# Even layer's out-projection on one Trainium2 core: operand blocks loaded by a casting DMA, low halves made by a negation and an adding DMA from GpSimd

## The chip, the cores and the metric

The kernel runs on one core of one Trainium2 chip. The metric is device time in microseconds, the median of several executions. The core's engines are named as in the profile: PE is TensorE (matmuls), PEld its weight loads, DVE VectorE, ACT ScalarE, POOL GpSimd and SP SyncE. A queue that issues DMAs is written with a q, as SPq.

## The reference, cut to what matters

The reference is a chain of four residual layers over one sequence of 1024 tokens with 1024 features in fp32: a gated linear recurrence (A), a latent attention (M), an even layer (E) and an odd layer (O), and a last normalisation. Layer E joins two branches and projects them back:

```
y_a = attn.reshape(b, s, DA_WIDTH) * silu(g_a)
...
y_b = rmsnorm(y, ssd_norm_w)
return concatenate([y_a, y_b], axis=-1) @ w_out
```

`y_a` comes from a differential attention, `y_b` from a state-space scan (SSD). Each has 1024 features, so `w_out` is 2048 by 1024 and its product is a sum of two parts: `y_a` by the upper half and `y_b` by the lower half. The change lies in how the blocks of `y_a` and `y_b` are brought into SBUF for this product.

## The kernel before, in words

**The matmul in three products.** TensorE multiplies operands of a rounded type, float32r (F32R in the code). To keep fp32 accuracy, every operand x is held as a high half, x rounded to float32r, and a low half, x minus that. `split` (line 545) makes them: ACT copies x into the high tile, which rounds it, and DVE subtracts the high tile from x into the low tile. A product is then three matmuls (`mm3`): high by high, high by low, low by high.

**The out-projection.** `out_proj` (line 853) takes the two parts with their sources in DRAM: `yA_d` for the attention, `yB_d` for the scan. Each is stored with 8 rows of 128 features, by 1024 tokens. The 1024 output features are done in four column groups c of 256. `PLANS` (line 802) gives each group a form: PPSS for the first part, PSSP for the second. P is a plain product (`plain`, line 889): four blocks, for output half b and token half h, of 8 row tiles by 3 matmuls, 24 matmuls each; the block for (b, h) = (0, 0) comes first, then (0, 1), (1, 0), (1, 1). S is a seven-product form on sums and differences of the operand blocks: 7 by 4 by 3, 84 matmuls. The sums are made from loads of their own (`load_sums`, tiles `tq`).

**The quads.** Both forms read quads. A quad is a quarter of the operand, 512 features by 512 tokens, as two pairs of tiles `yh` (high) and `yl` (low), each tile 128 partitions by 2 rows by 512 tokens. `load_quad` (line 804) loads one:

```
E.sync.dma_start(out=b.bitcast(F32), in_=src[k:k + 2, :, hs(h)].rearrange("k p s -> p k s"))
split(a, b, b.bitcast(F32))
```

So the fp32 block, 512 KB, lands in the tile `b` of the low half, ACT rounds it into `a`, and DVE subtracts in place. A part's first P needs all four quads, in the order (0,0), (1,0), (0,1), (1,1) of feature half and token half, which is 8 tile pairs. The first S of a part drops quad (0,1), and the last P of the second part loads it again, 2 more pairs. In all `load_quad` runs its inner body 8 + 8 + 2 = 18 times. No other layer calls it.

**What sets the order.** The kernel is written as a list of operations; `schedule` (line 296) plays them through a model of the engines and writes out a fixed order for every engine, so each engine runs its instructions strictly in that order and waits on semaphores. An operation's place follows from when its inputs are ready in the model, and among ready ones from its place in the list. `price` (line 253) gives a DMA 460 ns on the engine that issues it, whichever that is; line 377 lets it land at the earliest 2 us later, all DMAs one after another at 330 bytes per ns. A tile is taken from its class when the first operation that writes it is placed (`can_alloc`, line 319). Tiles `yh`, `yl`, `xr` and those of the scan share the class `c4`, 38 slots of 4 KB per partition; `yh` and `yl` have at most 16 each.

**Around the change.** SP issues all DMAs of the kernel before. POOL has few instructions: the additions of squares (`sumsq`, line 613) where the planner gives them to it, into `gacc` for the scan's normalisation and `acc` for the next layer's, and the power -1/2 behind every normalisation (`far_rstd`, line 582, and `next_norm`, line 644). The scan's result reaches `yB_d` only behind such a power. Every instruction is issued at line 431, so the profile names that line for all, and they are told apart by tile names: `ops` is the PSUM tile of the out-projection, `mm`, `yo`, `tp` those of the scan, `xr` the residual stream to which DVE adds each finished `ops`.

Of the kernel before, what the change touches and what calls it, by code (L numbers as in the profile page):

```python
# [10 lines left out]
F32 = mybir.dt.float32  # L11
F32R = mybir.dt.float32r
AF = mybir.ActivationFunctionType
ALU = mybir.AluOpType
# [420 lines left out]
def tile_kernel(ctx: ExitStack, tc: tile.TileContext, A, cc, out, stages="AMEO", dump=False):  # L435
    nc = tc.nc
    N4, N2, NW, NX = 38, 12, 9, 24
    E = Program()
# [3 lines left out]
    hs = lambda h: slice(h * HALF, (h + 1) * HALF)  # L442
# [102 lines left out]
    def split(hi, lo, src):  # L545
        splits((hi, lo, src))

    def splits(*items):
        for hi, lo, src in items:
            E.scalar.copy(hi, src)  # L550
        for hi, lo, src in items:
            E.vector.tensor_tensor(out=lo, in0=src, in1=hi.bitcast(F32), op=ALU.subtract)
# [251 lines left out]
    def load_quad(src, kq, h):  # L804
        hi, lo = [], []
        for j in range(2):
            a, b = T("yh", [128, 2, HALF], F32R), T("yl", [128, 2, HALF], F32R)
            k = kq * 4 + j * 2
            E.sync.dma_start(out=b.bitcast(F32), in_=src[k:k + 2, :, hs(h)].rearrange("k p s -> p k s"))
            split(a, b, b.bitcast(F32))  # L810
            hi.append(a)
            lo.append(b)
        return hi, lo
# [39 lines left out]
    def out_proj(parts, kind, near={}):  # L853
# [45 lines left out]
        for pi, (w_ap, nk, src) in enumerate(parts):  # L899
# [20 lines left out]
            def need(*which):  # L920
                for q in which:
                    if q not in quads:
                        quads[q] = load_quad(src, *q)
# [777 lines left out]
```

## Time and profile before

| | before |
|---|---|
| median of 3 executions | 2289.41 us (2288.76 to 2289.72) |
| the profiled execution's own time | 2289.98 us |
| its span, first to last instruction | 2288.2 us |
| PE busy | 2268.0 us |
| DVE busy | 1644.9 us |
| ACT busy | 1340.7 us |
| POOL busy | 113.8 us |
| granted TensorE clock, mean | 0.999 of full speed |
| DMA queue of SP | 207.92 MB, 28.7% of 16 engines' span |

Matmuls are pipelined and their ends are modelled, so PE counts as busy from a matmul's start to its modelled end: gaps shorter than the overlap don't show. The span is 1.8 us shorter than the execution's own time. The out-projection of layer E lies between about 1720 and 1900 us of the span; its loads begin at about 1670 us.

### The profile page before, as it was taken

What the parts mean: (1) busy time and instruction counts of PE and PEld (TensorE: products, weight loads), DVE (VectorE), ACT (ScalarE), POOL (GpSimd) and SP (SyncE); (2) the same over time, 40 slices, a digit from 0 to 9 for tenths busy, and PEclk for the clock granted to TensorE, in tenths of its full rate; (3) what the DMA queues carried; (4) which work ended last, traced back from release to release, by engine and by line L of the source; (5) the groups of instructions that cost most, each with busy time, mean ns of one, the idle gap of its engine ahead of it and who ended that gap; (6) DMA issues with size and microseconds to landing.
All of it is one profiled execution on the core that took longest, in us unless ns stands there. A gap on an engine that the chain in (4) does not pass through costs nothing.

```text
span 2288.2 us, 33162 instructions
## 1 busy us (share of the span) xinstructions
PE 2268.0 (99%) x11994; PEld 1917.2 (84%) x11994; DVE 1644.9 (72%) x3784; ACT 1340.7 (59%) x2778; POOL 113.8 (5%) x145
## 2 busy tenths in 40 slices
PE   8999999999999999999999999999999999999998
PEld 7888888888999888889898888878887878888887
DVE  7677944455777855976776757887879966777875
ACT  6666823433666744576666757586543435777852
POOL 0000011000000001000000000000000021000000
PEclk9999999999999999999999999999999999999999
DMA  6122423222111512312111121263336523111241
GB/s 224 60 80 86 170 88 92 65 97 90 47 53 58 188 65 59 120 38 56 48 48 47 51 60 43 56 173 93 111 131 213 191 74 113 47 56 47 95 164 74
DMA packets 181549, 210.04 MB, mean 92 GB/s; under 512 B 24729, under 2 KB 131445, under 8 KB 181385
## 3 DMA queue, kind: packets, MB, share of 16 engines
q1 hardware_dynamic: 181385, 207.92, 28.7%
q8 instruction: 94, 1.54, 0.3%
q14 instruction: 70, 0.57, 0.1%
HBM read 159.50 MB, written 46.28 MB: 90 GB/s over the span
## 4 chain that ended last, share of the span: by engine, by line
PE 96%; DVE 1%; DMA 1%; issue 1%; ACT 0%; SPq 0%; DVEq 0%; POOLq 0%; POOL 0%; ACTq 0%
PE mm L431 53%; PE ops L431 19%; PE sc L431 8%; PE ov L431 6%; PE tps L431 4%; PE yo L431 1%; PE mg L431 1%; PE tp L431 1%; PE nps L431 1%; DMA xT_d<-xe 0%; DMA csb<-cs_d 0%; PE aux L431 0%; DVE yl L431 0%; PE ftp L431 0%; SPq L431 0%
## 5 line engine op out<-in xcount | busy, mean ns | idle before, releaser
L431 PE MATMUL mm<-hT,whi 128*128 128x512 f32 (+1 forms) x3136 | 1001.4, 394 | 0.7 <-ACT hT L431 0.5
L431 PEld LDWEIGHTS mm<-hT,whi 128*128 128x128 f32 x3136 | 578.7, 188 | 119.4 <-issue 1.0
L431 PE MATMUL mm<-hT,wlo 128*128 128x512 f32 (+1 forms) x1568 | 616.3, 394 | 0.0
L431 PEld LDWEIGHTS mm<-hT,wlo 128*128 128x128 f32 x1568 | 294.9, 188 | 62.0 <-issue 1.4
L431 ACT ACTIVATE s<-s,st 128x257 f32<-128x257 f32 (+9 forms) x467 | 301.0, 663 | 73.3 <-DVE st L431 71.2
L431 PE MATMUL ops<-yh,whi 128*128 128x512 f32 x528 | 207.7, 396 | 0.6 <-DVE xr L431 0.6
L431 PE MATMUL ops<-yl,whi 128*128 128x512 f32 x528 | 208.1, 395 | 0.2 <-DVE yl L431 0.2
L431 PE MATMUL ops<-yh,wlo 128*128 128x512 f32 x528 | 207.9, 395 | 0.0
L431 DVE TENSOR_TENSOR pl<-tps,ph 128x512 fp32r<-128x512 f32 (+2 forms) x284 | 143.3, 536 | 79.1 <-ACT ph L431 77.3
L431 ACT CAST ph<-tps 128x512 fp32r<-128x512 f32 (+2 forms) x284 | 120.6, 469 | 106.8 <-PE tps L431 104.8
L431 DVE CUSTOM_DVE_ANT_0 s<-sc,bt 128x256 f32<-128x256 f32 (+3 forms) x320 | 149.6, 493 | 40.1 <-PE sc L431 37.2
L431 DVE TENSOR_TENSOR wlo<-raw,whi 128x512 fp32r<-128x512 f32 (+5 forms) x246 | 160.9, 673 | 21.6 <-ACT whi L431 15.9
L431 PE MATMUL ov<-ph,v 128*128 128x256 f32 (+2 forms) x700 | 159.7, 285 | 0.0
L431 DVE TENSOR_TENSOR xr<-ops,xr 128x512 f32<-128x512 f32 x108 | 74.2, 688 | 111.1 <-PE ops L431 110.9
L431 ACT CAST whi<-raw 128x512 fp32r<-128x512 f32 (+5 forms) x246 | 136.3, 582 | 20.1 <-DVE wlo L431 14.4
L431 PE MATMUL tps<-ident,s 128*128 128x128 f32 x816 | 135.2, 273 | 0.0
L431 PEld LDWEIGHTS ov<-ph,v 128*128 128x128 f32 x700 | 118.2, 189 | 9.8 <-ACT ph L431 1.6
L431 PEld LDWEIGHTS ops<-yh,whi 128*128 128x128 f32 x528 | 99.2, 188 | 24.1 <-DVE xr L431 1.0
L431 PEld LDWEIGHTS ops<-yl,whi 128*128 128x128 f32 x528 | 99.2, 188 | 23.6 <-DVE yl L431 0.6
L431 PEld LDWEIGHTS ops<-yh,wlo 128*128 128x128 f32 x528 | 99.1, 188 | 23.1
L431 PE MATMUL ov<-pl,v 128*128 128x256 f32 (+1 forms) x380 | 116.9, 308 | 0.2 <-DVE pl L431 0.2
L431 PEld LDWEIGHTS tps<-ident,s 128*128 128x128 f32 x816 | 99.2, 140 | 11.9
(318 smaller groups left out, 3999.3 us busy)
## 6 DMA issues: line engine op xcount, KB each, us to landing
raw<-in_w_in_a_dram SPq DMA_DIRECT2D x72, 512.0 KB
yl<-yA_d SPq DMA_DIRECT2D x48, 256.0 KB
raw<-in_w_out_a_dram SPq DMA_DIRECT2D x24, 512.0 KB
xr<-xT_d SPq DMA_DIRECT2D x24, 512.0 KB
raw<-in_w_in_c_dram SPq DMA_DIRECT2D x18, 512.0 KB
xT_d<-xr SPq DMA_DIRECT2D x32, 256.0 KB
yA_d<-y SPq DMA_DIRECT2D x32, 256.0 KB
csb<-cs_d SPq DMA_DIRECT2D x16, 512.0 KB
```

Source lines behind the costliest of these rows:

```text
L431: getattr(getattr(nc, op.eng), op.method)(*[conv(a) for a in op.args], **{k: conv(v) for k, v in op.kwargs.items()})
```

## The change

In `load_quad` alone, three lines replace two. The block is loaded by a DMA that GpSimd issues, from DRAM in fp32 into the high tile `a`, which has the type float32r, so the DMA casts. ACT writes the negative of `a` into the low tile `b`, with a Copy of scale -1. A second DMA of GpSimd reads the same block from DRAM again and adds it to `b`. DVE has no part in it any more.

```
--- before.py
+++ after.py
@@ -806,8 +806,10 @@
         for j in range(2):
             a, b = T("yh", [128, 2, HALF], F32R), T("yl", [128, 2, HALF], F32R)
             k = kq * 4 + j * 2
-            E.sync.dma_start(out=b.bitcast(F32), in_=src[k:k + 2, :, hs(h)].rearrange("k p s -> p k s"))
-            split(a, b, b.bitcast(F32))
+            y = src[k:k + 2, :, hs(h)].rearrange("k p s -> p k s")
+            E.gpsimd.dma_start(out=a, in_=y)
+            E.scalar.activation(b, a.bitcast(F32), AF.Copy, scale=-1.0)
+            E.gpsimd.dma_start(out=b, in_=y, accum_op=ALU.add)
             hi.append(a)
             lo.append(b)
         return hi, lo
```

The tile that is written first is now `a` where it was `b`.

## Rows read from the trace of the kernel before

**Rows 1.** The page, part 1: busy us, share of the span, instructions.

```profile
PE 2268.0 (99%) x11994; PEld 1917.2 (84%) x11994; DVE 1644.9 (72%) x3784; ACT 1340.7 (59%) x2778; POOL 113.8 (5%) x145
```

**Rows 2.** Windows: us, then PE, PEld, DVE, ACT, POOL busy, PEclk, DMA share, GB/s.

```profile
0.00:50.00 50.00, 41.12 (x298) 38.59 (x299) 36.19 (x99) 34.89 (x68) 4.93 (x20) 1.00 0.75 255
...
1700.00:1900.00 200.00, 198.22 (x915) 159.69 (x914) 165.90 (x250) 85.46 (x134) 21.17 (x15) 1.00 0.45 150
...
2250.00:2300.00 50.00, 31.15 (x135) 24.93 (x133) 19.53 (x38) 8.69 (x24) 3.54 (x7) 0.94 0.20 74
```

**Rows 3.** Tile views of yl and yh, 1660 to 1900 us: min/median/max ns.

```profile
L431 ACT CAST yh<-yl x18: 1031/1048/1053, 1700.8 to 1859.8; 128x1024 fp32r<-128x1024 f32 x18
L431 DVE TENSOR_TENSOR yl<-yl,yh x18: 1215/1220/1227, 1703.5 to 1862.3; 128x1024 fp32r<-128x1024 f32 x18
...
L431 SPq DMA_DIRECT2D yl<-yB_d x10: 359/371/1187, 1769.8 to 1831.6; - x10
```

**Rows 4.** Chain of waits, 1741 to 1831 us: start, us, what.

```profile
1741.67 88.06 PE ops L431 x379
```

**Rows 5.** Timeline of ACT, first part's roundings: start, us, instruction, idle before.

```profile
1710.38 2.93 ACT L431 CAST yh<-yl 128x1024 fp32r<-128x1024 f32 x3
...
1721.43 1.05 ACT L431 CAST yh<-yl 128x1024 fp32r<-128x1024 f32 x1
```

**Rows 6.** Timeline of PEld, out-projection's start: 1st, 7th and 43rd load of part one.

```profile
1720.29 0.19 PEld L431 LDWEIGHTS ops<-yh,whi 128*128 128x128 f32 x1
...
1721.57 0.19 PEld L431 LDWEIGHTS ops<-yh,whi 128*128 128x128 f32 x1
...
1736.65 0.19 PEld L431 LDWEIGHTS ops<-yh,whi 128*128 128x128 f32 x1
```

**Rows 7.** Timeline of SP, the second part's quad loads.

```profile
1769.77 0.89 SPq L431 DMA_DIRECT2D yl<-yB_d  x2
...
1793.71 4.54 SPq L431 DMA_DIRECT2D yl<-yB_d  x5
...
1799.37 1.19 SPq L431 DMA_DIRECT2D yl<-yB_d  x1
```

**Rows 8.** Timeline of ACT, the second part's roundings; in brackets the idle time and its end.

```profile
1793.49 1.05 ACT L431 CAST yh<-yl 128x1024 fp32r<-128x1024 f32 x1 [2.80 <-PE ops L431]
1794.88 1.05 ACT L431 CAST yh<-yl 128x1024 fp32r<-128x1024 f32 x1 [0.35 <-PE ops L431]
...
1797.81 1.05 ACT L431 CAST yh<-yl 128x1024 fp32r<-128x1024 f32 x1 [1.35 <-DMA yl<-yB_d]
...
1804.93 1.05 ACT L431 CAST yh<-yl 128x1024 fp32r<-128x1024 f32 x1 [0.96 <-DMA yl<-yB_d]
```

**Rows 9.** Timeline of DVE, second part: additions of the first two finished blocks.

```profile
1817.85 0.68 DVE L431 TENSOR_TENSOR xr<-ops,xr 128x512 f32<-128x512 f32 x1
...
1823.27 0.68 DVE L431 TENSOR_TENSOR xr<-ops,xr 128x512 f32<-128x512 f32 x1
```

**Rows 10.** Windows again, columns as in Rows 2: two stretches full of DMAs.

```profile
1715.00:1720.00 5.00, 4.88 (x24) 3.72 (x23) 5.00 (x6) 3.90 (x6) 0.00 (x0) 1.00 1.03 419
...
1800.00:1805.00 5.00, 5.00 (x23) 4.06 (x22) 3.72 (x4) 2.17 (x3) 0.00 (x0) 1.00 1.04 373
```

**Rows 11.** Timelines of POOL, then SP: sums, a power, the store of yB_d.

```profile
1734.18 1.49 POOL L431 TENSOR_TENSOR gacc<-gacc,sq 128x512 f32<-128x512 f32 x1 [31.90 <-ACT sq L431]
...
1745.37 1.02 POOL L431 TENSOR_TENSOR r<-r,mhalf 128x4 f32<-128x4 f32 x1 [7.12 <-DVE r L431]
...
1756.31 5.37 SPq L431 DMA_DIRECT2D yB_d<-yb  x8
```

## The prediction, made blind

> **What bounds the kernel now.** The page's table of engines comes first: PE is busy for 2268.0 of 2288.2 us, DVE for 72% of the span, POOL for 5% [rows 1]. The windows say where PE's missing 20.2 us lie: 8.9 in the first 50 us, 7.1 in the last 38, and only 1.8 in the 200 us that hold the out-projection, all of it at a granted clock of 1.00 [rows 2]. The chain of waits shows the same from the other side: one run of 379 matmuls in 88.06 us without a wait, 0.2323 us each [rows 4]. So PE sets the end in this stretch, and DVE, busy for 165.9 of those 200 us, is close behind but hidden. Whatever the change takes from DVE can return at most the 1.8 us in which PE stood idle; whatever it makes PE wait is added in full, since matmuls at 0.2323 us each leave nothing to catch up with.
>
> **What it removes.** 18 subtractions of 1.22 us leave DVE, 22.0 us in all [rows 3]. Worth: between 0 and 1.8 us, as above; I take 1.8, since the idle time lies where DVE is full [rows 2]. 18 DMA issues leave SP, 0.36 to 1.19 us each [rows 3]. SP's loads of weights and sums behind them may go out earlier; they are prefetches, so I count 0.
>
> **What it replaces.** ACT's 18 roundings of 1.05 us [rows 3] become 18 negations of the same shape. I take the same 1.05, a gain or loss of 0. What changes is the place: the negation waits for the casting DMA, as the rounding waited for the plain one, and ACT's later work queues behind it.
>
> **What it adds.** The old chain for a tile pair was DMA, ACT 1.05, DVE 1.22. The new one is casting DMA, ACT 1.05, adding DMA. The adding DMA can't start before ACT has finished, so a whole transfer takes the place of 1.22 us, and the operand blocks cross the DMA engines twice: 36 transfers of 512 KB where 18 were. The trace has no DMA from POOL, none that casts and none that adds, so both prices are bounded. From below: DMA engines that are full move 419 GB/s [rows 10], 1.25 us for 524288 bytes. From above, if only one is under way at a time: a quad load issued at 1793.71 released ACT by 1797.81 [rows 7, 8], 4.1 us, and a second stream (the adding DMA also reads its target) 2.4 us more, 6.5 us. The nearest rows are the second part's own loads of the same blocks: ACT was released at 1797.81 and, three loads later, at 1804.93 [rows 8], 2.4 us each. I take 2.4 for the casting DMA and 1.5 times that, 3.6, for the adding one, half way between one stream and two.
>
> The Trainium skill, in "DMA: Bandwidth & Descriptors", section "Anatomy of one DMA — SWDGE (gpsimd) path", gives 2.0 us plus the bytes over 436 GB/s for a DMA that GpSimd generates: as an estimate 3.2 us here alone, and 1.2 for each further one where the fixed part overlaps. By that the second part's sum below would be 14 times 1.2 plus 2, so no stall, or 14 times 3.2, so a stall of 17 us less the cover; no run here shows which.
>
> **First part: late or not.** PE takes up the first tile pair at 1720.29, the second (7th weight load) at 1721.57 and the eighth (43rd) at 1736.65 [rows 6]. ACT's second rounding starts at 1710.38 and the eighth ends at 1722.48 [rows 5]. With negations at the same places, the second adding DMA can start at about 1711.4, and seven of them at 3.6 us end at 1736.6: just in time, 0 us. At the lower bound they wait for ACT; at the upper one they end at 1756.9, 20 us late. In the way are the loads of `xr`: the DMA engines are full here as it is [rows 10].
>
> **Second part: this is where I expect the loss.** Its blocks can only be loaded into slots that the first part's last S form gives free. Two slots were free early, and two loads went out at 1769.77; six more at 1793.71 to 1800.6 [rows 7], after ACT had waited for PE's last use of old tiles [rows 8]. In the new kernel the two early slots go to the high tiles, so two casting DMAs are done early, but everything else, 6 casting and 8 adding DMAs, starts at about 1793.5. PE's first block ended by 1817.85 and its second by 1823.27 [rows 9]; 24 matmuls take 5.6 us [rows 4], so the first began near 1812.1, and the eighth tile pair (19th matmul of the second block) was needed at about 1821.8. That leaves 28.3 us. The transfers need 8 times 3.6 and 6 times 2.4, 43.2 us: 14.9 us late. The planner counts DMAs one after another as well, so it will put a block that reads the early quads, output half 1 by token half 0, in between: 24 matmuls, 5.6 us of cover. Stall 9.3 us.
>
> **The reload** of quad (0,1), two tile pairs for the last P form, is rounded by ACT between 1858 and 1862, the second pair by 1862.3 on DVE [rows 3]. It is outside the rush; two adding DMAs, 7.2 us, delay nothing that I can see: 0, and at 6.5 us each still under 10 us in a stretch of 60 us of PE work that doesn't read it.
>
> **POOL's queue.** POOL gets 36 DMA issues between its own instructions, and a waiting one holds those behind it: an adding DMA waits for ACT, and behind it stand the last sums of squares at 1734.18 and the power at 1745.37, which lead to the store of `yB_d`, issued by 1761.7 [rows 11]. Up to 1793.5, when the slots come free, that chain has 31.8 us to spare, and eight adding DMAs end at 1736.6 by my price: 0 us.
>
> **The sum.** 9.3 of new stall less 1.8 given back is 7.5 us. On the profiled execution's 2289.98 us, which is 0.6 us above the median of the runs shown, this gives 2297.5 us.
>
> **Rivals.**
> - *The transfers keep pace* (35%). With casts at 2.4, the second part fits its 28.3 us and the 5.6 of cover if an adding DMA takes 2.4 us or less, the pace of a plain load. For it: DMA engines at 419 GB/s would need 1.25 us per stream, and the windows after 1805 have room. Then only DVE's relief is left, 2288.2 to about 2290 us.
> - *Adding DMAs cost two streams or more, or run one at a time* (17%). At 4.8 us, twice 2.4, the first part ends at 1745.0, 8.4 late, 2.8 after the cover of one block; the second needs 52.8 us, 24.5 late, 18.9 after cover. With 1.8 back, 2310 us; the upper bounds (6.5 and 4.1) give some 2347.
> - *POOL becomes the bound* (5%). If issues waiting on slots or on ACT hold POOL past 1777, the power comes over 31.8 us late, the `yB_d` chain reaches PE, and each further us is a us lost: 2300 us for 10.
> - *Faster by over 0.2%* (3%). It would take 4.6 us, and PE idles only 4.2 us outside the first 50 and last 38 us of the span. Only another order of the whole plan could do it: about 2284 us.
>
> That the casting DMA doesn't round, or that the low half comes out as zero, would cost accuracy and leave the matmuls and these times as they are.
>
> **How the numbers follow.** The forecast has 40%; its own range, for adding DMAs of 3.2 to 4.2 us, is 2294 to 2303. A difference of 0.2%, 4.6 us, is about what a measurement of this kernel can tell from none. Slower by more: all but 5 of the forecast's 40, with 17 and 5 from the second and third rival, 0.57. Within 0.2%: 35 and 5, 0.40. Faster: 0.03. The range runs from 2287.5, all of DVE's relief and no stall, to 2322, the second rival half way to its bounds; it leaves out the slow end of the one-at-a-time case and the faster plan.
>
> **What would show it.** In the changed kernel's chain of waits, PE's long run of `ops` should break near 1812 to 1830, with DMAs into `yl` as what ended the idle time; the windows there should show the DMA engines full. ACT should show waits on DMAs into `yh`, DVE 22 us less work, POOL 36 issues. I am wrong if PE's busy time stays within 2 us of 2268 and the time with it (the transfers keep pace), if the largest gap lies before 1745 (the first part), or if `yl` is in time and PE waits for something behind POOL.

## The result and the profile after

The changed kernel takes 2346.90 us (median of 4, 2346.65 to 2351.78), before 2289.56 on the same chip: 1.025 times as long, interval 1.0238 to 1.0262, or 57.3 us more. The forecast was 2297.5 with a range up to 2322. The profiled execution took 2351.78 us, 4.9 above the median.

The page of the changed kernel: its span and engines (columns as in [rows 1]):

```profile
span 2350.0 us, 33202 instructions
...
PE 2287.0 (97%) x11994; PEld 1928.1 (82%) x11994; DVE 1624.4 (69%) x3767; ACT 1340.5 (57%) x2778; POOL 147.7 (6%) x180
```

And its DMA queues, the page's third part (packets, MB, share of sixteen engines over the span):

```profile
q1 hardware_dynamic: 176489, 198.49, 26.6%
q0 software_dynamic: 9792, 18.88, 3.8%
```

DVE has lost 20.5 us of work: the 18 subtractions, less one addition of squares that the planner now gives to DVE in place of POOL. ACT has the same as before. POOL has 35 instructions more and a DMA queue of its own, q0, with the 36 new transfers. The span is 61.8 us longer, and 19.0 of these are PE being busy longer. The rest is waiting, as the waits of PE between 1700 and 1960 us show (who waited for whom: us in total, times, longest; `nps` is the PSUM tile of the scan's normalisation, `sqh` its rounded sum of squares, which comes behind POOL's additions, and `whi` the high half of the weights):

```profile
PE ops L431 <- DMA yl<-yB_d: 19.4, 6, 6.4
PE nps L431 <- ACT sqh L431: 12.0, 2, 11.8
PE ops L431 <- ACT whi L431: 4.4, 1, 4.4
PE ops L431 <- DMA yl<-yA_d: 3.8, 1, 3.8
```

With three smaller groups this is 44.3 us, where PE stood idle for 1.8 us in the 200 us of [rows 2]. Where the waits come from is seen on POOL. Its timeline in the second part:

```profile
1862.42 1.21 POOL L431 DMA_DIRECT2D yl<-yB_d  x1 [8.94 <-issue]
1869.18 1.21 POOL L431 DMA_DIRECT2D yl<-yB_d  x1 [5.55 <-ACT whi L431]
1875.94 1.19 POOL L431 DMA_DIRECT2D yl<-yB_d  x1 [5.56 <-issue]
1882.76 1.20 POOL L431 DMA_DIRECT2D yl<-yB_d  x1 [5.63 <-issue]
```

The tile view of `yl`, 1862 to 1895 us, says when these four adding DMAs landed:

```profile
L431 POOL DMA_DIRECT2D yl<-yB_d x4: 1189/1200/1206, 1862.4 to 1882.8; - x4
...
DMA to landing us min/median/max: 6.4/6.5/6.5
```

An adding DMA lands 6.4 to 6.5 us after its issue, and the next starts 6.8 us after the one before: one at a time. POOL idles 5.6 us in between. ACT can't be what it waits for, since the last negation before these issues started at 1853.25 and took 1.06 us; the profile finds no releaser ("issue") for two of the three gaps. Nor are the DMA engines the reason, as the window of the four shows (columns as in [rows 2]):

```profile
1862.40:1889.20 26.80, 16.35 (x48) 11.68 (x48) 7.02 (x12) 2.50 (x4) 4.80 (x4) 0.82 0.52 80
```

They are busy for 0.52 of 26.8 us, 3.5 us for each adding DMA, and idle for the rest. (80 GB/s over 26.8 us is 2.1 MB, the four blocks and little else.)

PE's 19.0 us of longer busy time are in part the clock. After the long gap in the first part it comes back slow. The window of those 10 us (columns as in [rows 2]):

```profile
1750.00:1760.00 10.00, 5.89 (x15) 4.54 (x15) 1.29 (x2) 2.84 (x5) 5.00 (x4) 0.53 0.46 89
```

And the timeline of PE there:

```profile
1754.11 0.79 PE L431 MATMUL nps<-sqh,ones_r 128*128 128x512 f32 x1 [11.76 <-ACT sqh L431]
...
1755.13 0.63 PE L431 MATMUL ops<-yh,whi 128*128 128x512 f32 x1
1755.56 0.63 PE L431 MATMUL ops<-yl,whi 128*128 128x512 f32 x1
```

The granted clock is 0.53 in this window, the lower level of 1.2 GHz, after PE had stood still for 11.76 us, and matmuls follow each other at 0.43 us, where [rows 4] has 0.23.

### The profile page after: what moved, and what is told of

Same layout as the page of the kernel before. It is cut to its first block, busy times and chain, and to the rows that moved or that the text cites. A ratio compares the mean times of both kernels' runs of the same rounds, so it can differ in the third digit from the quotient of the medians.

```text
span 2350.0 us, 33202 instructions
## 1 busy us (share of the span) xinstructions
PE 2287.0 (97%) x11994; PEld 1928.1 (82%) x11994; DVE 1624.4 (69%) x3767; ACT 1340.5 (57%) x2778; POOL 147.7 (6%) x180
## 4 chain that ended last, share of the span: by engine, by line
PE 90%; issue 5%; DMA 2%; DVE 1%; POOL 1%; SPq 0%; ACT 0%; POOLq 0%; DVEq 0%; ACTq 0%
PE mm L431 51%; PE ops L431 16%; PE sc L431 8%; PE ov L431 6%; PE tps L431 4%; PE yo L431 1%; PE mg L431 1%; PE tp L431 1%; PE nps L431 1%; POOL yl L431 1%; SPq L431 0%; DMA xT_d<-xe 0%; DMA csb<-cs_d 0%; PE aux L431 0%; POOL yh L431 0%
## 5 line engine op out<-in xcount | busy, mean ns | idle before, releaser
L431 ACT ACTIVATE sq<-xr 128x512 f32<-128x512 f32 x58 | 36.6, 631 | 135.0 <-DVE xr L431 128.9
```

Of the source, the lines that this page charges most:

```text
L431: getattr(getattr(nc, op.eng), op.method)(*[conv(a) for a in op.args], **{k: conv(v) for k, v in op.kwargs.items()})
```

## The experiments

Three theories stood against each other from the trace: that POOL has room for only one adding DMA at a time (R), that the move itself takes 6.5 us (M), and that POOL waits for ACT in the order that the planner wrote (Q). The expectations put the room down to descriptors, the entries that are written for a transfer; the runs vary the room and don't show what fills it. The kernel sets a scratch size for such DMAs itself, `dynamic_dma_scratch_size=1024`, and R takes that for the room. The ratios are to the kernel before, run beside each version, with medians of 2290.5 to 2291.2 us.

**More room.** The changed kernel, with one number altered:

```
-    nc = bacc.Bacc("TRN2", ..., dynamic_dma_scratch_size=1024)
+    nc = bacc.Bacc("TRN2", ..., dynamic_dma_scratch_size=4096)
```

> The changed kernel with a DMA scratch of 4096 bytes per partition in place of 1024, nothing else. In the changed kernel POOL issues the adding DMAs 6.4 to 6.8 us apart and sits idle in between for nothing that the profile names, while the DMA engines are only half busy. Theory R (the room for descriptors: an adding DMA fills more than half of it, so one is under way at a time, and POOL waits for the one before to land): with four times the room they overlap, each then costs what the DMA engines are busy for it, about half of 6.8, 3.4 us; the time falls from 2347 to between 2292 and 2312. Theory M (the move itself takes 6.5 us, and they run one after another whatever the room): 2340 to 2350. Theory Q (POOL waits for ACT, in the order the planner wrote): 2340 to 2350 too, with POOL's waits put down to ACT.

Measured: 2304.94 us, 1.0065 times before (1.0042 to 1.0088). 42 of the 57 us are gone. POOL's timeline in the second part's rush:

```profile
1809.15 1.20 POOL L431 DMA_DIRECT2D yl<-yB_d  x1 [3.81 <-ACT yl L431]
1814.93 1.20 POOL L431 DMA_DIRECT2D yl<-yB_d  x1 [4.58 <-ACT yl L431]
1817.34 1.19 POOL L431 DMA_DIRECT2D yl<-yB_d  x1 [1.22 <-ACT yl L431]
1819.10 1.18 POOL L431 DMA_DIRECT2D yl<-yB_d  x1 [0.57 <-ACT yl L431]
```

Now they follow at down to 1.8 us, and what POOL waits for is ACT's negation. That 6.5 us is the move's own time is out, and so is Q in this form: both would have left the time as it was. A smaller step of the same number:

> The changed kernel with a DMA scratch of 2048 bytes. With 1024 the time is 2347 (adding DMAs one at a time), with 4096 it is 2305 (DMA engines full, POOL never idle for an unnamed reason). If the room for descriptors is a count of transfers (theory R), twice the room lets two or three adding DMAs overlap, which at a landing time of 6.5 us and 3.3 us of movement each nearly fills the DMA engines: 2305 to 2320, much nearer to 4096 than to 1024. If the gain with 4096 came from other addresses in SBUF or from the plan, 2048 should give no ordered step: 2335 or more is against theory R.

Measured: 2308.27 us (1.0088, 1.0059 to 1.0117). Twice the room brings most of the gain, as R had it. POOL still idles for an unnamed reason in places, here 4.90 us, where the kernel with 4096 has at most 0.3 us of it before an issue in the rush:

```profile
1828.96 1.18 POOL L431 DMA_DIRECT2D yl<-yB_d  x1 [4.90 <-issue]
```

**Cut the adding DMA in two**, with the room of 1024:

```
-            E.gpsimd.dma_start(out=b, in_=y, accum_op=ALU.add)
+            for n in range(2):
+                E.gpsimd.dma_start(out=b[:, n], in_=src[k + n, :, hs(h)], accum_op=ALU.add)
```

> The changed kernel, scratch 1024, with each adding DMA of two rows cut into two of one row, 256 KB each. Theory R: each half takes half the room, so two or three halves are under way at once and the cost per block falls from 6.6 to some 4 to 5 us: 2305 to 2330. Theory M: the same bytes at the same pace, 2343 to 2352, or later by the second DMA's fixed part.

Measured: 2318.63 us (1.0122, 1.0093 to 1.0151). The same bytes in the same room, in smaller pieces, save 28 us.

The traces say more on the room than these times, if issue and landing of every DMA of POOL are put side by side. Count an adding DMA of 512 KB as two and every other (casting, plain, or adding half a block) as one: then with 1024 never more than 3 are under way, in any run, and with 2048 never more than 7, while with 4096 there are up to 11 and no such wait. In the changed kernel 23 stretches of POOL's idle time, 101.5 us in all, end 0.3 us after the landing of an earlier DMA of POOL, whatever the profile names as releaser. What fills the room isn't shown by this: the profiles' pages count the same 272 packets for an adding and for a casting DMA (4896 over 18, below), and 144 for a plain one (2592 over 18).

**Each half of the change alone.** Casting DMA only, in place of the negation and the adding DMA:

```
+            E.sync.dma_start(out=b.bitcast(F32), in_=y)
+            E.vector.tensor_tensor(out=b, in0=b.bitcast(F32), in1=a.bitcast(F32), op=ALU.subtract)
```

> Half of the change: the casting DMA of POOL writes the high tile, SP loads the same block in fp32 into the low tile as before, DVE subtracts in place; no negation, no adding DMA. Theory R: a casting DMA is smaller in descriptors and nothing waits for two transfers in a row, so the operand is in time as before: 2286 to 2296. Against it (any DMA that POOL issues comes late): 2300 or more.

Measured: 2294.87 us (1.0018, 1.0007 to 1.0029). And the adding DMA only, with

```
-            E.gpsimd.dma_start(out=a, in_=y)
+            E.sync.dma_start(out=a.bitcast(F32), in_=y)
+            E.scalar.copy(a, a.bitcast(F32))
```

> The other half: SP loads the block in fp32 into the high tile, ACT rounds it in place and writes its negative into the low tile, POOL's adding DMA adds the block; no casting DMA. Theory R: the adding DMAs alone hold the time, 2332 to 2347. Against it (casting DMAs, which share the room and POOL's queue, carry a third or more of the loss): 2295 to 2328.

Measured: 2351.35 us (1.0265, 1.0234 to 1.0296), all of the loss, and above the range by 4 us. Each of the two has 18 DMAs of POOL of one kind, so their pages price the kinds (columns as above). Casting only, span 2293.3 us:

```profile
q0 software_dynamic: 4896, 9.44, 1.4%
```

Adding only, span 2347.1 us:

```profile
q0 software_dynamic: 4896, 9.44, 2.5%
```

That is 1.4% of 2293.3 us over 18, 1.8 us of all sixteen engines for a casting DMA, and 2.5% of 2347.1 over 18, 3.3 us for an adding one. A landing of 6.5 us is thus about half movement.

**POOL as the issuer, nothing else.** In the kernel before, `E.sync` becomes `E.gpsimd` for the quads' loads:

> The kernel before with one edit: the quads' plain loads are issued by POOL in place of SP; no cast, no adding DMA, ACT rounds and DVE subtracts as before, scratch 1024. It prices the move of 18 DMAs to POOL alone. Theory R: a plain transfer is small in room, nothing follows it but ACT: 2288 to 2293. Against it (POOL's DMAs come late whatever they do): 2298 or more.

Measured: 2291.75 us (1.0005, 0.9996 to 1.0015): no difference that can be told from none. The move to POOL alone isn't the loss. Its queue, span 2287.7 us:

```profile
q0 software_dynamic: 2592, 9.44, 1.2%
```

Over 18 that is 1.5 us of all sixteen engines for a plain DMA of POOL.

**Each part alone.** The new lines under `if src is yA_d`, the old ones in the other branch, and the same with `yB_d`:

> The change on the first part's blocks alone (attention, 8 tile pairs); the second part's 10 tile pairs are loaded as before. In the changed kernel the first slots for the second part come free at 1821.3 us, before at 1793.5: my prediction had 0 for this part, the trace says some 28 us. If the two parts' losses add, this gives 2310 to 2320. If the first part's delay is only carried forward into a wait that the second part has anyway, under 2300.

Measured: 2311.32 us (1.0089, 1.0054 to 1.0124), 20.8 us over before.

> The change on the second part's blocks alone (scan, 10 tile pairs). If the losses add, the rest of the 57 us: 2315 to 2328. By the rival (one wait that both parts share), 2340 or more.

Measured: 2322.44 us (1.0138, 1.0101 to 1.0174), 31.9 us over. Together 52.7 of the 57.3: the losses add, nearly.

**POOL's own work out of the way.** The scan's sums of squares stay on DVE (the planner's choice of GpSimd is dropped for them; the argument `alt` is new in `sumsq`):

```
-                    sumsq(acc[h], y[:, hs(h)], hq == 0)
+                    sumsq(acc[h], y[:, hs(h)], hq == 0, alt=False)
```

> The changed kernel, scratch 1024, with the scan's four sums of squares fixed to DVE, so that nothing on the way to the scan's normalisation but its two powers stands in POOL's queue. In the changed kernel PE waited 12 us for the tiles that follow from those sums, which stood behind adding DMAs on POOL. Theory Q (POOL's order makes a loss of its own): up to 12 us less, 2333 to 2341. Theory R alone (those 12 us only hide a wait for the operand that comes next): 2343 to 2350.

Measured: 2350.89 us (1.0262, 1.0221 to 1.0303), nothing gained. The waits of PE in this kernel, 1650 to 1990 us:

```profile
PE ops L431 <- DMA yl<-yA_d: 14.5, 4, 6.5
PE ops L431 <- DMA yl<-yB_d: 13.9, 6, 4.9
...
PE nps L431 <- ACT sqh L431: 2.5, 1, 2.5
```

The wait for `sqh` has gone from 12.0 to 2.5 us, and the wait for the first part's low tiles has come up from 3.8 to 14.5. So the 12 us behind POOL's queue had only covered a wait for the operand, as far as this kernel can tell, whose order the planner wrote anew. That the sums behind POOL's waiting issues cost the time by themselves (Q as this run states it) falls.

**What is left with room enough.** With 4096, some 14 us remain. The windows of the rush, 1800 to 1840 us, of the kernel before and of the one with 4096, in this order:

```profile
1800.00:1840.00 40.00, 39.83 (x172) 31.87 (x171) 37.88 (x54) 22.52 (x36) 3.11 (x2) 1.00 0.49 167
```

```profile
1800.00:1840.00 40.00, 31.93 (x121) 24.09 (x120) 16.92 (x27) 14.84 (x22) 11.02 (x11) 0.91 1.10 264
```

The DMA share is up from 0.49 to 1.10, full, at fewer GB/s than the 419 of [rows 10]. If that is the reason, fewer bytes to add must help (scratch 4096 kept):

```
-            E.gpsimd.dma_start(out=b, in_=y, accum_op=ALU.add)
+            E.gpsimd.dma_start(out=b[:, 0], in_=src[k, :, hs(h)], accum_op=ALU.add)
```

> Scratch 4096 as before, and each adding DMA covers only the first of its two rows (256 KB); the second row of the low half stays at the negative of the high half, so that half of the low-half correction is left out. With scratch 4096 some 15 us of loss are left. Theory D (what is left is the DMA engines' time: the windows show them full, and 18 adding DMAs take 3.3 us of all sixteen each): half the bytes give back half of the adding DMAs' 26 us in the second part's rush, and the time comes down to 2290 to 2298. Theory L (what is left is the chain of two landings with ACT between, whatever the size): 2300 to 2305.

Measured: 2292.39 us (1.0010, 1.0000 to 1.0020). The same window:

```profile
1800.00:1840.00 40.00, 37.82 (x159) 29.22 (x158) 27.59 (x44) 22.10 (x35) 11.25 (x14) 1.00 0.86 234
```

The chain of casting DMA, ACT and adding DMA is as long in steps as before, so it wasn't the number of landings: with enough room, the size of the adding DMAs decides. How isn't separated: the engines are less full, and half a block also lands sooner by itself, 3.7 us after the issue for the first one of this run, where the whole block took 6.0 with 4096. Last, whether room was also the 4 us of the casting half:

> The casting DMA alone (SP loads the fp32 block into the low tile, DVE subtracts) with scratch 4096. With 1024 it measured 2294.9, 0.18% above before, and POOL idled 2.8 us for room. If that room was the 4 us: 2289 to 2292. If it is the extra load of every block (18 transfers more on DMA engines that are full there) or the plan: 2293 to 2296. Neither theory expects it faster than before by more than 2 us.

Measured: 2295.89 us (1.0019, 1.0010 to 1.0028). POOL's waits for room are gone in this kernel (with 1024 they came to 14.1 us by the count above, of which the profile left 2.8 unnamed), and the time isn't better: it wasn't the room. Whether it is the extra load or the plan was not tried. No version here is faster than the kernel before, and PE's 1.8 us of idle time say why none could be by much.

## Why the prediction was wrong

**The bound** was right. PE sets the end, and 20.5 us less work on DVE bought nothing that can be seen: even the run with half the adding, which has DVE at 1624.5 us as well, is no faster than before.

**ACT at the same price** was right: the negations take 1.054 us (median), the roundings took 1.048 [rows 3].

**The price of the adding DMA** is the step that failed: "1.5 times that, 3.6, for the adding one, half way between one stream and two". As a time of the DMA engines 3.6 is good, 3.3 was measured. But I let seven of them follow each other at that price, as SP's loads of [rows 8] do, and in this kernel one had to land before the next began: 6.3 to 6.8 us where nothing else was in the way. That was my bound from above, "if only one is under way at a time", and nothing in the trace of before spoke against it, since it has no DMA of POOL. I gave the case 17% and cut the range off half way to it. The casting DMA's 2.4 had the same fault: 1.8 was measured on the engines, but with an adding DMA under way only one casting DMA had room beside it. The code had a hint that I didn't price, the scratch of only 1024.

The Trainium skill gives, in "DMA: Bandwidth & Descriptors", section "Anatomy of one DMA — SWDGE (gpsimd) path", 2.0 us plus bytes over 436 GB/s, an estimate of 3.2 us for these blocks. No landing here is that short, and the measurement decides: an adding DMA takes 6.0 us at the least, a casting one in the changed kernel 4.1, and a plain one of POOL 3.9. The Trainium skill, in the section "SWDGE vs HWDGE vs iDMA" of "DMA: Bandwidth & Descriptors", says that GpSimd writes descriptors into rings, which the DMA engines drain packet by packet. The runs with 2048 and 4096 fit that, since with more scratch more of POOL's DMAs are under way; that it is the count of descriptors which fills it, and how many an adding DMA writes, was not measured.

**The first part in time** was wrong by 20.8 us (the change on that part alone). By my bound from above it was 20 us late, 14.4 after the cover of a block that can go ahead. **The second part's 9.3** were 31.9. With the bounds from above I had 42.7 there. With 14.4 for the first part and 1.8 given back that makes 2345.3 us, where the second rival says "some 2347". That either is near the measured 2346.90 is to some degree chance, since one part came out higher and the other lower.

**POOL's queue at 0** was right in the sum, though not in the picture. The last two sums did slip, the first of them from 1734.18 [rows 11] to 1751.66, and PE did wait for them, but without that wait it would have waited for the operand, by the run with the sums on DVE. The power slipped from 1745.37 to 1777.41, and the store of `yB_d` held the two early casting DMAs until 1796.03; the slots for the others came free later still, at 1821.34, when PE was done with the first part's late tiles.

**The reload at 0** was right: its adding DMAs are issued at 1920.97 and 1929.31, and PE is busy without a gap from 1910 to 1940.

**The signs.** Two that I named went against the mechanism. The largest gap, 11.76 us, begins at 1742.35, in the first part, where I expected none. And the DMA engines were not full behind PE's waits for `yl`: 0.52 in the window of the four adding DMAs, 0.87 from 1830 to 1862, where casting DMAs and other loads ran beside them.

**Slower than the sum of the waits.** That a gap also costs matmuls at the lower clock afterwards was in no term of mine. It is part of the 19.0 us.

## What to carry to other kernels

A DMA that GpSimd issues takes room in the scratch, and in these runs an adding one took as much as two plain or casting ones of the same block: before moving transfers to GpSimd, look at how much scratch the program reserves, and price them one at a time unless a run shows them overlapping. A transfer that must wait for another transfer, in a place where buffers come free late, lengthens the wait of the engine that reads the result, and work taken from an engine that isn't the bound (here 20.5 of DVE's 1644.9 us) doesn't pay for it. When an operation is absent from a trace, the case at the far bound is a rival with full weight, and the range has to reach it.

## What the runs showed of the hardware

- An adding DMA of 512 KB keeps the sixteen DMA engines busy for about 3.3 us, a casting one for about 1.8 and a plain one of POOL for about 1.5; at the peak rate of [rows 10] the same bytes take 1.25.
- POOL is held 1.19 to 1.23 us by the issue of an adding DMA and 0.72 to 0.77 by a casting one (1189/1216/1232 and 716/738/767 ns min/median/max in the second part), while SP's issues took 0.37 (median in [rows 3]).
- With a scratch of 1024, POOL had at most one adding DMA of 512 KB under way with one casting DMA beside it, or three that were plain, casting or adding of 256 KB; with 2048, at most three adding ones with one casting DMA beside them.
- While POOL waits for room, the profile often names no releaser, only "issue", and sometimes an instruction of ACT that had nothing to do with it, as `whi` above: a wait whose length repeats (5.1 to 5.6 us) while its releaser changes, and which ends 0.3 us after an earlier DMA of POOL has landed, is worth reading as one wait.
- After 11.76 us without a matmul the granted clock was 0.53, and matmuls came at 0.43 us instead of 0.23.
